# Scores of the 1024 noisy keys in one two-bank PSUM tile: PSUM as two double tiles and four single banks

## The chip, the cores and the metric

The kernel runs on one core of one Trainium2 chip. A time is the device time of one execution in microseconds (us). TensorE (PE) does the matrix products and the transposes, VectorE (DVE), ScalarE (ACT) and GpSimd (POOL) the rest, and SyncE (SP) issues the DMAs. PE writes its results to PSUM, which has eight banks of 512 float32 numbers in each of 128 partitions; DVE and ACT read them from there.

## The reference

A two-layer transformer trunk: 1024 noisy tokens (`x`) and 256 context tokens (`ctx`), width 1024, in float32. Each layer is a mixer with two kinds of attention heads, an output projection, and a SwiGLU of hidden width 2816. The part that matters here:

```
s = einsum('bqhgd,bkhd->bhgqk', q, k) * scale      # keys: 256 context and 1024 noisy ones
p = softmax(s, axis=-1)
o = einsum('bhgqk,bkhd->bqhgd', p, v)
...
s = einsum('bqhid,bkhid->bhiqk', q, k) * d ** -0.5 # differential heads: two streams i
p = softmax(s, axis=-1)
a = p[:, :, 0] - lam * p[:, :, 1]
...
g, u = split(h @ w_in, 2); y = (silu(g) * u) @ w_out
```

Layer 0 has eight windowed heads with sinks (A) and eight latent heads over all 1280 keys (B). Layer 1 has eight grouped heads (C) and four differential heads (D), both over all 1280 keys.

## The kernel before

Activations lie feature by feature, in chunks of tokens: `a` and `b` (512 noisy tokens each) and `c` (256 context tokens, layer 0 only). Every float32 operand is split into a high and a low float32r part, and a product is three matmuls (`mm3`).

**The order.** The program is first recorded by `Recorder` (L51). It then issues the instructions as a list schedule orders them: each engine takes, of the instructions whose operands are there, the first in program order, with estimated times and with the number of buffers of each pool counted (`room`, L196). This fixes each engine's order at build time. The tile framework then sets every wait: a reader waits for the writers of its tile, a later writer for the readers before it, and a new tile for the last readers of the buffer that it gets.

**PSUM.** Before, one pool `pb` (L283) has eight tiles of one bank each; `pr.b()` (L309) takes one. Who takes them:

- `Proj.run` (L783): 24 matmuls into one bank, then an ACT copy.
- Attention, a `Job` (L792) of up to four query tiles of 128. `scores` (L842) makes, per query tile and stream, three pieces (noisy keys 0 to 511, 512 to 1023, context keys), each in its own bank with its own DVE maximum (`piece`, L852); a small DVE maximum joins the three. `ex` (L867) then makes three ACT exponentials with sums. Windowed jobs (`s_local`, L935) use a bank of up to 384 columns and one of 256 per query tile.
- `pv_steps` (L988): for each of ten key tiles four transposes of probabilities into a bank (`tr`), an ACT cast to the high part, a DVE subtraction for the low part (`low`), and two products with the values into the job's output bank, which is held for the whole job.
- `g_ada` (L437): one bank is held over 32 matmuls that are spread beside the attention.
- `gu` (L1631): for hidden tile j and chunk c, 24 matmuls into a bank for g and 24 into another for u. ACT takes Silu of g and DVE multiplies it with u. `down` (L1649): eight banks in turn, three matmuls each, and a DVE addition to the running sum from each.

The full-key jobs are 16 of B, 8 of D (two streams each) and 16 of C: 192 score steps. `gu` runs 22 times for each chunk: 66 times in layer 0 (a, b, c), 44 in layer 1 (a, b).

Of the kernel before, what the change touches and what calls it, by code (L numbers as in the profile page):

```python
# [32 lines left out]
# columns of the packed per-partition parameters  # L33
# [17 lines left out]
class Recorder:  # L51
    """Stands for nc while the program is laid out. The instructions are then issued as a list schedule orders them:
    an engine that is free takes, of the instructions whose operands are there, the first in program order.
    Times are estimates that only decide the order; Tile sets every wait."""
# [27 lines left out]
    def boxes(ap):  # L82
        """Tile name and the boxes (rows, columns) that ap covers."""
# [44 lines left out]
    def record(self, k, f, name, args, kw):  # L128
# [46 lines left out]
        # from the engine of the row to the engine of the column  # L175
# [87 lines left out]
class FM:  # L263
    """Feature-major activations of one token chunk: [128, KT, n] over 4 KB tiles."""
# [11 lines left out]
class Prog:  # L276
    def __init__(self, ctx, nc, tc, d, out):
# [5 lines left out]
        self.pb = ctx.enter_context(tc.tile_pool(name="pb", bufs=8, space=bass.MemoryType.PSUM))  # L283
        self.dp = ctx.enter_context(tc.tile_pool(name="dp", bufs=1, space=bass.MemoryType.DRAM))
        for p, n in (("sp", 24), ("tp", 44), ("up", 13), ("pb", 8)):
            nc.pool(p, n)
# [24 lines left out]

    def dram(self, shape, dt=F32R):
        return self.dp.tile(shape, dt, name=self.nm("scr"))
# [90 lines left out]
    def mm3(self, ps, terms):  # L404
        """sum over terms (whi, wlo, xhi, xlo) of w^T x."""
# [6 lines left out]
    def wsplit(self, raw, w=1024):  # L412
        """The first w columns of a weight tile, split."""
# [23 lines left out]
    def g_ada(self, l, g, ahead=2):  # L437
        """The 2048 modulation columns of group g."""
# [37 lines left out]
    def derive(self, l, g):  # L476
        """Scales and gates with the norms' gains: A1, G1, A2, G2 per feature and stream."""
# [28 lines left out]
        # first guess from the exponent, then three Newton steps  # L506
# [8 lines left out]
    def expand(self, cols):  # L515
        """Columns [128, w], each 64 times in a row."""
# [5 lines left out]
    def bcast(self, cols, g=1):  # L522
        """Token columns [128, nt * g] to rows: [128, n tokens] in PSUM."""
# [8 lines left out]
    def sq_add(self, acc, x, n, k):  # L532
        """x^2, the k-th term, to the sums acc (one on Pool, a second one on DVE)."""
# [17 lines left out]
    def g_modnorm(self, x, n, A, Bv, put, acc=None, w=1):  # L551
        """rms-normalised x times A plus B, split; A(kt), B(kt) are per-partition columns."""
# [1299 lines left out]
```

## Time and profile before

| | |
|---|---|
| median of 3 runs | 3406.78 us (3404.93 to 3407.7) |
| profiled execution, span from first to last instruction | 3405.7 us |
| PE busy | 3302.8 us (97%) |
| DVE busy | 2079.6 us (61%) |
| ACT busy | 1398.0 us (41%) |
| POOL busy | 697.2 us (20%) |

The profiled execution is told by its span; what lies around the span is not shown, and its 3405.7 us lie inside the range of the runs. A busy PE in such a profile is one whose modelled matmul records leave no gap. The stages as read from the trace: start, norms and projections of layer 0 up to about 295 us, windowed attention (A) to 467, latent attention (B) to 746, output projection, norms and SwiGLU of layer 0 to about 1720, projections of layer 1 to 2100, differential attention (D) to 2308, grouped attention (C) to 2554, output projection and SwiGLU of layer 1 to the end.

### The profile page before, as it was taken

What the parts mean: (1) busy time and instruction counts of PE and PEld (TensorE: products, weight loads), DVE (VectorE), ACT (ScalarE), POOL (GpSimd) and SP (SyncE); (2) the same over time, 40 slices, a digit from 0 to 9 for tenths busy, and PEclk for the clock granted to TensorE, in tenths of its full rate; (3) what the DMA queues carried; (4) which work ended last, traced back from release to release, by engine and by line L of the source; (5) the groups of instructions that cost most, each with busy time, mean ns of one, the idle gap of its engine ahead of it and who ended that gap; (6) DMA issues with size and microseconds to landing.
All of it is one profiled execution on the core that took longest, in us unless ns stands there. A gap on an engine that the chain in (4) does not pass through costs nothing.

```text
span 3405.7 us, 45603 instructions
## 1 busy us (share of the span) xinstructions
PE 3302.8 (97%) x16916; PEld 2687.9 (79%) x16916; DVE 2079.6 (61%) x4013; ACT 1398.0 (41%) x3200; POOL 697.2 (20%) x1059
## 2 busy tenths in 40 slices
PE   7989999999999999999998999999999999999997
PEld 5865588887888888888877895678887788888886
DVE  5565588875534444444468745898994545444545
ACT  4365688874411111111134324788994411111111
POOL 2311221125200000000044723682114200000003
PEclk8999999999999999999999999999999999999998
DMA  6266442354201111111123346412145211111111
GB/s 236 81 236 229 167 132 72 98 193 160 80 28 42 44 38 38 38 38 38 38 95 136 105 133 194 130 52 71 60 163 176 68 56 38 56 43 51 56 56 62
DMA packets 134446, 325.56 MB, mean 96 GB/s; under 512 B 12432, under 2 KB 34640, under 8 KB 134224
## 3 DMA queue, kind: packets, MB, share of 16 engines
q1 hardware_dynamic: 134224, 322.65, 28.8%
q8 instruction: 133, 2.18, 0.3%
q14 instruction: 89, 0.73, 0.1%
HBM read 243.63 MB, written 71.63 MB: 93 GB/s over the span
## 4 chain that ended last, share of the span: by engine, by line
PE 82%; DVE 8%; POOL 3%; DMA 3%; ACT 2%; issue 2%; POOLq 0%; SPq 0%; DVEq 0%; ACTq 0%
PE b L260 82%; DVE T L260 3%; DVE U L260 3%; DVE S L260 2%; POOL S L260 2%; POOL U L260 1%; ACT T L260 1%; DMA scr<-T 1%; ACT U L260 1%; DMA T<-in_ada_w_dram 1%; DMA U<-scr 1%; POOL T L260 0%; DMA T<-in_ctxT_dram 0%; POOLq L1847 0%; DMA T<-scr 0%
## 5 line engine op out<-in xcount | busy, mean ns | idle before, releaser
L260 PE MATMUL b<-T,T 128*128 128x512 f32 (+5 forms) x9958 | 2170.5, 367 | 23.1 <-DVE T L260 9.6
L260 PEld LDWEIGHTS b<-T,T 128*128 128x128 f32 (+2 forms) x9958 | 1714.3, 190 | 378.9 <-issue 27.9
L260 PE MATMUL b<-U,T 128*128 128x512 f32 (+2 forms) x3808 | 946.0, 381 | 9.4 <-DVE U L260 4.4
L260 PEld LDWEIGHTS b<-U,T 128*128 128x128 f32 x3808 | 661.6, 190 | 135.6 <-issue 12.8
L260 POOL TENSOR_TENSOR U<-U,U 128x512 f32<-128x512 f32 (+1 forms) x130 | 174.9, 1349 | 1696.5 <-ACT U L260 1692.2
L260 DVE TENSOR_TENSOR T<-T,b 128x512 f32<-128x512 f32 (+1 forms) x872 | 501.6, 631 | 11.4 <-PE b L260 6.5
L260 DVE TENSOR_TENSOR T<-T,T 128x1024 fp32r<-128x1024 f32 (+4 forms) x274 | 316.7, 1170 | 227.3 <-PE b L260 172.9
L260 DVE TENSOR_REDUCE S<-b 128x1 f32<-128x512 f32 (+1 forms) x672 | 377.3, 571 | 116.2 <-PE b L260 111.0
L260 DVE TENSOR_TENSOR U<-U,b 128x512 f32<-128x512 f32 (+1 forms) x118 | 75.2, 637 | 608.4 <-PE b L260 605.5
L260 ACT ACTIVATE T<-b,S 128x512 f32<-128x512 f32 (+1 forms) x640 | 390.6, 616 | 53.5 <-DVE S L260 36.0
L260 ACT CAST T<-T 128x1024 fp32r<-128x1024 f32 (+4 forms) x234 | 225.1, 968 | 360.8 <-PE b L260 296.4
L260 DVE TENSOR_TENSOR U<-b,U 128x512 fp32r<-128x512 f32 (+3 forms) x528 | 335.6, 648 | 21.2 <-ACT U L260 16.8
L260 ACT ACTIVATE U<-b 128x256 f32<-128x256 f32 (+1 forms) x148 | 81.3, 552 | 620.8 <-PE b L260 618.8
L260 ACT CAST U<-b 128x512 fp32r<-128x512 f32 (+3 forms) x528 | 295.7, 572 | 97.4 <-PE b L260 90.4
L260 PE MATMUL b<-ident,T 128*128 128x128 f32 x1968 | 314.3, 276 | 6.3 <-DVE U L260 2.5
L260 PEld LDWEIGHTS b<-ident,T 128*128 128x128 f32 x1968 | 239.7, 141 | 76.0 <-ACT T L260 9.3
L260 ACT CAST U<-U 128x512 fp32r<-128x512 f32 (+1 forms) x110 | 63.6, 578 | 305.1 <-DVE U L260 300.9
L260 POOL TENSOR_TENSOR T<-T,T 128x512 f32<-128x512 f32 (+2 forms) x104 | 132.5, 1282 | 175.6 <-ACT T L260 162.4
L260 PE MATMUL b<-T,silc 128*32 128x512 f32 x384 | 131.8, 626 | 11.0 <-DMA T<-in_ada_w_dram 10.5
L260 DVE TENSOR_TENSOR U<-U,U 128x512 fp32r<-128x512 f32 (+4 forms) x167 | 118.9, 713 | 38.2 <-POOL U L260 27.1
L260 ACT ACTIVATION_READ_ACCUMULATOR T<-b,S 128x1 f32 x640 | 136.6, 213 | 0.0
L260 ACT ACTIVATE U<-T 128x512 f32<-128x512 f32 (+1 forms) x174 | 96.4, 578 | 96.1 <-DVE T L260 90.4
(71 smaller groups left out, 1514.5 us busy)
## 6 DMA issues: line engine op xcount, KB each, us to landing
scr<-T SPq DMA_DIRECT2D x114, 512.0 KB
T<-in_ada_w_dram SPq DMA_DIRECT2D x96, 512.0 KB
T<-in_ffn_in_dram SPq DMA_DIRECT2D x88, 512.0 KB
T<-scr SPq DMA_DIRECT2D x82, 512.0 KB
T<-scr SPq DMA_DIRECT2D x88, 256.0 KB
T<-in_ffn_out_dram SPq DMA_DIRECT2D x44, 512.0 KB
T<-in_w_out_dram SPq DMA_DIRECT2D x32, 512.0 KB
T<-scr SPq DMA_DIRECT2D x72, 128.0 KB
```

What stands on the lines that cost most here:

```text
L260: f(*args, **kw)
```

## The change

The scores with the 1024 noisy keys go to one tile of two banks, with one DVE maximum over 1024 columns and one ACT exponential over 1024 columns; the context scores keep a single bank. To make room, PSUM becomes a pool `pb` of four single banks and a pool `pw` of two double tiles. `Proj.run` now takes a double tile (and uses half of it), and `gu` puts g and u into the two halves of one double tile. All else takes single banks, as before: transposes, output sums, context and windowed scores, `down`, `g_ada`, the norms.

```diff
-        self.pb = ctx.enter_context(tc.tile_pool(name="pb", bufs=8, space=bass.MemoryType.PSUM))
+        self.pb = ctx.enter_context(tc.tile_pool(name="pb", bufs=4, space=bass.MemoryType.PSUM))
+        self.pw = ctx.enter_context(tc.tile_pool(name="pw", bufs=2, space=bass.MemoryType.PSUM))
...
+    def w(self):
+
+        return self.nc.tile("pw", self.pw.tile([P, 1024], F32, tag="w", name=self.nm("w")))
...
-            ps = pr.b()
+            ps = pr.w()
...
-        parts = (("x", 0, 512), ("x", 512, 1024), ("c", 0, 256)) if self.full else (("c", 0, 256),)
...
+        def x(h):
+            if h == 0:
+                own["s"] = pr.w()
+            self.mms(si, qi, "x", h * 512, h * 512 + 512, own["s"][:, h * 512:h * 512 + 512])
+            if h == 0:
+                return None
+            return lambda: nc.vector.tensor_reduce(out=m[:, mo:mo + 1], in_=own["s"], axis=AX.X, op=ALU.max)
+
+        def ctx():
+            s = own["sc"] = self.mms(si, qi, "c", 0, 256)
...
+            last = i == int(full)
+            nc.scalar.activation(own["c"] if last else own["x"], own.pop("sc") if last else own.pop("s"), AF.Exp,
+                                 bias=neg, accum_out=z[:, zo + i:zo + i + 1])
...
+        if full:
+            return [lambda: x(0), lambda: x(1), ctx], [lambda: ex(0), lambda: ex(1)]
...
-        ps = {}
-        for kind in "gu":
+        ps, both = {}, pr.w()
+        for i, kind in enumerate("gu"):
             wh, wl = self.conv[kind, j]
-            ps[kind] = pr.b()[:, :n]
+            ps[kind] = both[:, i * 512:i * 512 + n]
```

The order of the built programs shows what else moves. The first place is PE at the middle of one `gu` of layer 0 with 512 tokens, where the matmuls of g end and those of u begin (`b` and `w` are PSUM tiles, the other names SBUF tiles). Before:

```order
L260 MATMUL b3061_3142<-T2525_2606,T3009_3090 128x512
L260 MATMUL b3061_3142<-T2529_2610,T3009_3090 128x512
L260 MATMUL b3061_3142<-T2525_2606,T3010_3091 128x512
L260 MATMUL b3062_3143<-T2522_2603,T3011_3092 128x512 [waits DVE_49]
L260 MATMUL b3062_3143<-T2526_2607,T3011_3092 128x512
L260 MATMUL b3062_3143<-T2522_2603,T3012_3093 128x512
```

The same place now:

```order
L260 MATMUL w2962_3046<-T2458_2542,T2913_2997 128x512
L260 MATMUL w2962_3046<-T2462_2546,T2913_2997 128x512
L260 MATMUL w2962_3046<-T2458_2542,T2914_2998 128x512
L260 MATMUL w2962_3046<-T2455_2539,T2915_2999 128x512
L260 MATMUL w2962_3046<-T2459_2543,T2915_2999 128x512 [waits Activation_49]
L260 MATMUL w2962_3046<-T2455_2539,T2916_3000 128x512
```

The second matmul of u has got a wait for ACT. Followed through the counts of the semaphores in the built program, the awaited instruction is the Silu that reads the first half of the same tile, and that Silu waits for the first matmul of u, the last PE write to the tile ahead of it in the order. Of the 110 runs of `gu`, 109 have such a wait inside their 48 matmuls: 87 with 512 tokens, 22 with 256 (there mostly at the third matmul of u). Before, none has.

The second place is PE in the windowed attention, around the job whose output bank is `b983` (`ident` marks transposes; `b894` is the bank of `g_ada`; 128x384 and 128x256 from two `T` tiles are windowed and context scores). Before:

```order
L260 MATMUL b984_1065<-T794_875,T797_878 128x384 [waits PE_49]
L260 MATMUL b984_1065<-T795_876,T797_878 128x384
L260 MATMUL b986_1067<-ident_75,T938_1019 128x128 [waits DVE_49]
L260 MATMUL b986_1067<-ident_75,T949_1030 128x128
L260 MATMUL b894_975<-T946_1027,silc_81 32x512 [waits DMAHW7_49]
L260 MATMUL b894_975<-T946_1027,silc_81 32x512
L260 MATMUL b983_1064<-U977_1058,T34_115 128x384 [waits Activation_49]
L260 MATMUL b894_975<-T947_1028,silc_81 32x512 [waits DMAHW0_49]
L260 MATMUL b989_1070<-T796_877,T797_878 128x256 [waits DVE_49]
```

Now:

```order
L260 MATMUL b983_1067<-U981_1065,T35_119 128x384 [waits Activation_49]
L260 MATMUL b984_1068<-T794_878,T797_881 128x384 [waits DVE_49]
L260 MATMUL b984_1068<-T795_879,T797_881 128x384
L260 MATMUL b983_1067<-U982_1066,T35_119 128x384
L260 MATMUL b986_1070<-ident_78,T938_1022 128x128 [waits Activation_49]
L260 MATMUL b986_1070<-ident_78,T949_1033 128x128
L260 MATMUL b989_1073<-T796_880,T797_881 128x256 [waits DVE_49]
L260 MATMUL b989_1073<-T796_880,T797_881 128x256
L260 MATMUL b983_1067<-U987_1071,T35_119 128x256 [waits Activation_49]
L260 MATMUL b990_1074<-ident_78,T949_1033 128x128 [waits DVE_49]
```

The matmuls of `g_ada` are gone from here (they stand earlier, closer together), and each new tile (`b984`, `b986`, `b989`, `b990`) waits for a reader of a tile that was written just ahead of it.

The third place is DVE in the grouped attention. Before, a score step has three wide maxima and a small one:

```order
L260 TENSOR_REDUCE S5537_5620<-b5545_5628 128x1 [waits PE_49]
L260 TENSOR_REDUCE S5481_5564<-S5480_5563 128x4 [waits Activation_49]
L260 TENSOR_TENSOR T5431_5514<-T5431_5514,b5548_5631 128x512 [waits PE_49]
L260 TENSOR_REDUCE S5537_5620<-b5549_5632 128x1 [waits PE_49]
L260 RECIPROCAL S4005_4088<-S5481_5564 128x4 [waits DVE_49]
L260 TENSOR_REDUCE S5537_5620<-b5554_5637 128x1 [waits PE_49]
L260 TENSOR_REDUCE S5536_5619<-S5537_5620 128x1 [waits DVE_49]
```

Now it has two and a small one:

```order
L260 TENSOR_REDUCE S5287_5373<-w5302_5388 128x1 [waits PE_49]
L260 TENSOR_TENSOR U5305_5391<-b5303_5389,U5304_5390 128x512 [waits Activation_49]
L260 TENSOR_REDUCE S5287_5373<-b5311_5397 128x1 [waits PE_49]
L260 TENSOR_TENSOR U5310_5396<-b5308_5394,U5309_5395 128x512 [waits Activation_49]
L260 TENSOR_REDUCE S5286_5372<-S5287_5373 128x1 [waits DVE_49]
```

One wide maximum per step is gone from DVE; the one that stays reads both banks (`w5302`).

## Rows read from the trace of the kernel before

**Rows 1.** The page: span, busy time by engine, then the chain that ended last.
```profile
span 3405.7 us, 45603 instructions
PE 3302.8 (97%) x16916; PEld 2687.9 (79%) x16916; DVE 2079.6 (61%) x4013; ACT 1398.0 (41%) x3200; POOL 697.2 (20%) x1059
...
PE 82%; DVE 8%; POOL 3%; DMA 3%; ACT 2%; issue 2%; POOLq 0%; SPq 0%; DVEq 0%; ACTq 0%
```

**Rows 2.** Busy time by stretch: A, B, most of D, C, both SwiGLU stages.
```profile
core 0: us, PE busy (x) PEld busy (x) DVE busy (x) ACT busy (x) POOL busy (x), PEclk, DMA share, GB/s
295.00:467.00 172.00, 167.04 (x873) 105.76 (x874) 107.03 (x367) 114.62 (x368) 44.24 (x73) 0.97 0.58 185
467.00:746.00 279.00, 276.34 (x1681) 236.17 (x1680) 233.75 (x486) 231.01 (x612) 46.29 (x51) 1.00 0.41 118
2145.00:2308.00 163.00, 159.76 (x842) 119.09 (x840) 153.68 (x383) 129.53 (x364) 134.07 (x196) 0.98 0.23 69
2308.00:2554.00 246.00, 242.40 (x1465) 202.65 (x1464) 227.32 (x470) 224.85 (x580) 41.64 (x58) 1.00 0.31 101
900.00:1720.00 820.00, 820.00 (x4306) 709.05 (x4306) 379.54 (x652) 142.65 (x215) 9.53 (x30) 1.00 0.12 40
2690.00:3355.00 665.00, 665.00 (x2946) 551.04 (x2945) 321.91 (x468) 120.07 (x159) 6.92 (x16) 1.00 0.16 50
```

**Rows 3.** Timeline, one gu and the start of its down, 512 tokens, layer 0.
```profile
start us, us, engine line op out<-in xcount [idle before <-releaser]
1202.61 11.07 PE L260 MATMUL b<-T,T 128*128 128x512 f32 x48
...
1208.28 0.60 ACT L260 ACTIVATE U<-b 128x512 f32<-128x512 f32 x1 [7.06 <-PE b L260]
...
1213.79 0.69 DVE L260 TENSOR_TENSOR U<-U,b 128x512 f32<-128x512 f32 x1 [10.03 <-PE b L260]
```

**Rows 4.** Timeline near 231 us: PE waits for an ACT read of PSUM.
```profile
231.34 0.58 ACT L260 COPY U<-b 128x512 f32<-128x512 f32 x1
...
231.97 0.96 PE L260 MATMUL b<-T,T 128*128 128x512 f32 x3 [1.43 <-ACT U L260]
```

**Rows 5.** Timeline of layer 1's SwiGLU: three running matmuls; casts around a Silu.
```profile
2903.82 0.84 PE L260 MATMUL b<-T,T 128*128 128x512 f32 x3
...
2913.43 1.05 ACT L260 CAST T<-T 128x1024 fp32r<-128x1024 f32 x1 [2.46 <-DVE T L260]
2915.58 0.60 ACT L260 ACTIVATE U<-b 128x512 f32<-128x512 f32 x1 [1.10 <-PE b L260]
```

**Rows 6.** Timeline of one down with 256 tokens, layer 0.
```profile
1199.73 3.04 PE L260 MATMUL b<-U,T 128*128 128x256 f32 x24
1200.35 0.42 DVE L260 TENSOR_TENSOR U<-U,b 128x256 f32<-128x256 f32 x1 [2.92 <-PE b L260]
1200.69 0.75 DVE L260 TENSOR_TENSOR T<-T,b 128x256 f32<-128x256 f32 x2
...
1201.35 0.42 DVE L260 TENSOR_TENSOR U<-U,U 128x256 fp32r<-128x256 f32 x1
1201.69 2.07 DVE L260 TENSOR_TENSOR T<-T,b 128x256 f32<-128x256 f32 x6
```

**Rows 7.** Groups by form, whole span: count, busy us, mean ns, idle before.
```profile
L260 ACT ACTIVATE T<-b,S 128x512 f32<-128x512 f32 x384 | 265.6, 697 | 47.9 <-DVE S L260 30.5 <-PE b L260 14.6 <-POOL T L260 0.9
L260 DVE TENSOR_REDUCE S<-b 128x1 f32<-128x512 f32 x384 | 261.4, 685 | 58.3 <-PE b L260 55.2
L260 ACT ACTIVATION_READ_ACCUMULATOR T<-b,S 128x1 f32 x640 | 136.6, 213 | 0.0
L260 ACT ACTIVATE T<-b,S 128x256 f32<-128x256 f32 x256 | 126.8, 495 | 5.6 <-DVE S L260 5.5
L260 DVE TENSOR_REDUCE S<-b 128x1 f32<-128x256 f32 x288 | 120.6, 419 | 57.8 <-PE b L260 55.8
L260 ACT ACTIVATE U<-b 128x256 f32<-128x256 f32 x32 | 12.3, 384 | 49.4 <-PE b L260 49.2
```

**Rows 8.** Groups by form, 2411 to 2553 us: output copies, one for each C job.
```profile
L260 ACT COPY U<-b 128x512 f32<-128x512 f32 x10 | 5.9, 591 | 1.9 <-PE b L260 1.9
```

**Rows 9.** Timeline in C: a bank of transposes, its cast, its subtraction.
```profile
2401.85 0.60 PE L260 MATMUL b<-ident,T 128*128 128x128 f32 x4
...
2402.53 0.63 ACT L260 CAST U<-b 128x512 fp32r<-128x512 f32 x1
...
2403.55 0.68 DVE L260 TENSOR_TENSOR U<-b,U 128x512 fp32r<-128x512 f32 x1
```

**Rows 10.** Groups by form, 444.3 to 467.4 us: output copies, one for each A job.
```profile
L260 ACT COPY U<-b 128x512 f32<-128x512 f32 x3 | 1.8, 587 | 1.4 <-PE b L260 0.8 <-issue 0.6
```

**Rows 11.** Timeline in A: transposes, context scores, and readers of PSUM tiles.
```profile
445.18 0.38 PE L260 MATMUL b<-ident,T 128*128 128x128 f32 x2
...
445.31 0.48 PE L260 MATMUL b<-T,T 128*128 128x256 f32 x2
...
445.40 0.55 DVE L260 CUSTOM_DVE_ANT_0 T<-b,U 128x384 f32<-128x384 f32 x1
445.42 0.47 ACT L260 CAST U<-b 128x384 fp32r<-128x384 f32 x1
...
445.94 0.55 DVE L260 TENSOR_TENSOR U<-b,U 128x384 fp32r<-128x384 f32 x1
445.98 0.47 ACT L260 ACTIVATE T<-b,S 128x256 f32<-128x256 f32 x1
```

More of the change, by code (lines that the diff above doesn't have):

```diff
@@ L847, in scores @@
         neg = self.neg[:, 8 * si + qi:8 * si + qi + 1]
-        parts = (("x", 0, 512), ("x", 512, 1024), ("c", 0, 256)) if self.full else (("c", 0, 256),)
-        np_ = len(parts)
+        full = self.full
         own = {}
-        def piece(i):
-            s = self.mms(si, qi, *parts[i])
-            st.append(s)
+        def x(h):
[5 more added lines that the diff above has]
+            return lambda: nc.vector.tensor_reduce(out=m[:, mo:mo + 1], in_=own["s"], axis=AX.X, op=ALU.max)
@@ L856, in mx @@
+        def ctx():
+            s = own["sc"] = self.mms(si, qi, "c", 0, 256)
             def mx():
-                if np_ == 1 and not self.sinks:
+                if not full and not self.sinks:
                     nc.vector.tensor_reduce(out=neg, in_=s, axis=AX.X, op=ALU.max, negate=True)
                     return
-                o = mo + i if np_ > 1 else mo + 1
-                nc.vector.tensor_reduce(out=m[:, o:o + 1], in_=s, axis=AX.X, op=ALU.max)
-                if i == np_ - 1:
-                    nc.vector.tensor_reduce(out=neg, in_=m[:, mo + (np_ == 1):mo + 3], axis=AX.X, op=ALU.max,
-                                            negate=True)
@@ L865, in piece, with place @@
-            return mx
+                nc.vector.tensor_reduce(out=m[:, mo + 1:mo + 2], in_=s, axis=AX.X, op=ALU.max)
+                o = mo if full else mo + 1
+                nc.vector.tensor_reduce(out=neg, in_=m[:, o:o + 2], axis=AX.X, op=ALU.max, negate=True)
+            return mx
+        def place():
+            if self.neglam is not None:
+                if si == 0:
+                    self.zd = pr.S()
+                own["z"], own["o"] = self.zd, 4 * si
+            else:
+                own["z"], own["o"] = self.z, 4 * qi
+            if si == 0:
+                own["x"] = pr.T() if full else None
+                self.pb.append(own["x"])
+                own["c"] = self.pc[:, qi * 256:(qi + 1) * 256]
+            else:
+                own["x"], own["c"] = pr.T(), pr.U()[:, :256]
@@ L867, in ex @@
         def ex(i):
-            kind, a, b = parts[i]
             if i == 0:
-                if self.neglam is not None:
-                    if si == 0:
-                        self.zd = pr.S()
-                    own["z"], own["o"] = self.zd, 4 * si
-                else:
-                    own["z"], own["o"] = self.z, 4 * qi
-                if si == 0:
-                    own["x"] = pr.T() if self.full else None
-                    self.pb.append(own["x"])
-                    own["c"] = self.pc[:, qi * 256:(qi + 1) * 256]
-                else:
-                    own["x"], own["c"] = pr.T(), pr.U()[:, :256]
@@ L882, in ex @@
-            z, zo = own["z"], own["o"]
-            nc.scalar.activation(own["x"][:, a:b] if kind == "x" else own["c"], st[i], AF.Exp, bias=neg,
-                                 accum_out=z[:, zo + i:zo + i + 1])
-            if i == np_ - 1:
-                st.clear()
-                if si == 1:
-                    self.combine(qi, own["x"], own["c"], z)
-        return [lambda i=i: piece(i) for i in range(np_)], [lambda i=i: ex(i) for i in range(np_)]
+                place()
+            z, zo = own["z"], own["o"]
@@ L892, in combine @@
+            last = i == int(full)
+            nc.scalar.activation(own["c"] if last else own["x"], own.pop("sc") if last else own.pop("s"), AF.Exp,
+                                 bias=neg, accum_out=z[:, zo + i:zo + i + 1])
+            if last and si == 1:
+                self.combine(qi, own["x"], own["c"], z)
+        if full:
+            return [lambda: x(0), lambda: x(1), ctx], [lambda: ex(0), lambda: ex(1)]
+        return [ctx], [lambda: ex(0)]
     def combine(self, qi, pb1, pc1, s):
@@ L895, in combine @@
         z = s[:, 8:10]
-        nc.vector.tensor_reduce(out=z, in_=s[:, 0:8].rearrange("p (s t) -> p s t", s=2)[:, :, 0:3], axis=AX.X,
+        nc.vector.tensor_reduce(out=z, in_=s[:, 0:8].rearrange("p (s t) -> p s t", s=2)[:, :, 0:2], axis=AX.X,
                                 op=ALU.add)
@@ L913, in sums @@
         if self.neglam is None:
-            w = 3 if self.full else 1 if self.local is None else 2
+            w = 1 if not self.full and self.local is None else 2
             if w == 1:
```

7 lines of the change are left out of this document (3 added, 4 removed).

## The prediction

> **What bounds the kernel now.** I read the page first: PE is busy for 3302.8 of 3405.7 us, and 82% of the chain that ended last is PE [rows 1]. Then the stretches, since the change touches stages with different limits [rows 2]. In the two SwiGLU stretches PE has no gap at all (820.00 of 820 and 665.00 of 665 us), while DVE is busy 46 to 48% and ACT 17 to 18% of them: there the time is PE's, DVE or ACT time that is saved gives nothing, and each wait put in front of a matmul costs its full length. In C all three engines are nearly full (PE 242.40, DVE 227.32, ACT 224.85 of 246 us). In D DVE leads (153.68 of 163 us in the part shown, much of the rest idle at its start). In A and B PE leads again, with DVE and ACT at 62 to 84%.
>
> **What is removed.** Each of the 192 full score steps loses one wide DVE maximum and one ACT exponential with its read of the sum. A maximum takes 0.685 us on 512 columns and 0.419 on 256 [rows 7], so a column costs about 1.04 ns and the start 0.15 us: one over 1024 columns is about 1.22 us, against 2 x 0.685. Saved: 0.15 us, 29 us in all. An exponential takes 0.697 and 0.495 us, and the read of its sum 0.213 [rows 7]: one over 1024 columns is about 1.10 + 0.21, against 2 x 0.91, so 0.51 us less, 98 us in all (less in place, since the read overlaps). That is the whole gift, and nearly all of it lies beside PE work. Only in D, where DVE sets the pace, can it come out directly: 64 steps x 0.15 = 10 us at most.
>
> **What is added in gu.** This is the largest term, and it stands in the order: PE may not issue the second matmul of u (the third with 256 tokens) before Silu has read g, and Silu itself waits for the first matmul of u. The stall is one round trip PE, ACT, PE. In the trace the 48 matmuls of a gu run in 11.07 us [rows 3]; with 0.39 us for one (three in a row take 0.84 [rows 5]) they start every 0.227 us. The 24th then ends at about 1208.23, and Silu starts at 1208.28: 0.05 us after it. Silu takes 0.60 us [rows 3]. Where PE waits for an ACT read of PSUM, it starts 0.05 us after that read ends (231.34 + 0.58 to 231.97), and its next three matmuls take 0.96 us where running ones take 0.84 [rows 4, 5]: 0.12 us for starting again. So the second matmul of u starts 0.39 + 0.05 + 0.60 + 0.05 = 1.09 us after the first instead of 0.227, and with the restart a gu of 512 tokens loses 0.98 us. With 256 tokens matmuls start every 0.12 us and last 0.28 (3.04 us for 24 [rows 6]), and an ACT read of 256 columns takes 0.384 [rows 7]: 0.28 + 0.05 + 0.38 + 0.05 - 0.12 + 0.12 = 0.76 us. The order has 87 and 22 of them: 85 + 17 = **+102 us**. Nothing lies beside it: the other accumulations of these stages come later in PE's order, and PE issues in order. Queued behind the waiting matmul are the rest of u and the down products; DVE's multiplication waits for these and is late by as much. Bounds: without the restart, and with handovers of 0.04, 0.83 x 87 + 0.62 x 22 = 86; if the weight casts of 1.05 us, which today end about a microsecond ahead of Silu [rows 5], hold it up once in ten times, 112.
>
> The Trainium skill, PSUM — Partial Sum Buffer (PSUM bank collisions raise a hardware error), says that two engines may use PSUM at the same time as long as they are in different banks, and g and u are in different banks of the double tile. By that rule alone this term is zero and the sum below ends near 3439. The rows of before agree with it, since there PE goes on with u while Silu reads g [rows 3]; but the order now has the wait, so I count by the order.
>
> **Down with four banks.** With 256 tokens a bank is filled every 0.36 us, and DVE frees one every 0.33 (six in 2.07 us, the last lasting 0.42), after a multiplication and with a subtraction between [rows 6]. With four banks the fifth fill (1.44 us after the start, at 1201.17) finds the first addition done (about 1201.1), the sixth (1201.53) the second, but the seventh (at 1201.89) needs the third addition, which starts at 1201.69 and takes 0.42: some 0.3 us of waiting, 22 times, **+6 us** (0 to 15). With 512 tokens a bank is filled every 0.69 us and an addition is as long, with half a microsecond to spare: nothing.
>
> **Attention with four single banks.** The output bank is held throughout, so three are left for scores and transposes (two while a group of g_ada runs).
>
> A: per job (three in 23.1 us, 7.7 us each [rows 10]) seven transposed tiles, four context and four windowed scores pass through them. A transposed tile is held for its transposes, cast and subtraction, 0.38 + 0.47 + 0.55 and three handovers, 1.55 us; context scores for matmuls, maximum, small maximum and exponential, about 0.48 + 0.42 + 0.15 + 0.47 + 0.2 = 1.7; windowed scores 1.1 [rows 7, 11]. Together 22.5 us of bank time, 7.5 us over three banks, if no reader is ever late. ACT and DVE are busy for most of the job, so some lateness is certain; a quarter more makes 9.4 us, 1.7 x 16 jobs = 27. PE's matmuls for g_ada fill part. I take **+18** (0 to 38).
>
> C: a job takes 14.2 us (ten in 142 [rows 8]). A transposed tile is held from 2401.85 to 2404.23, 2.4 us [rows 9]; context scores, for which the exponential of the 1024 comes first, about 3.8 us by the durations above. 14.2 for the output, 4 x 3.8 and 10 x 2.4 make 53 of the 57 us of bank time that four banks have in a job: 94% full, and the readers' longest pieces have grown to 1.2 and 1.3 us. Against it stand 2 us of ACT and 0.6 us of DVE less per job, of some 13 of each (227 and 225 of 246 us [rows 2]). I take 0.5 us more per job, **+8** (-10 to +20).
>
> B: the same bank time in jobs of about 16 us, 86% full: **+2** (-8 to +12). D: jobs of 26 us leave room, except while g_ada holds a bank; DVE's saving against that: **-4** (-10 to +10).
>
> **The rest.** Proj.run takes two double tiles where eight were free; a tile takes 5 us to fill and its ACT copy 0.6, so two are enough, except where norms still deliver. The norms hold a single bank for their broadcast while down runs on the others. **+4** (0 to 12).
>
> Sum: 102 + 6 + 18 + 8 + 2 - 4 + 4 = 136; 3405.7 + 136 = 3541.7, and as the median of the runs is 1.1 us above the profiled span, 3542.
>
> **The rivals.**
> 1. *The wait in gu costs nothing and the saving counts: faster.* Its place is the second matmul of u, its price zero if Silu's end never comes after that matmul's turn. For it: the saving in D and C is real, 10 + 10 us, and if bank waits stay at their low bounds (0 in A, -8 in B) the time is 3407 - 28 = 3379. Against it: Silu alone takes 2.6 matmul intervals [rows 3] and starts after a matmul that PE has just issued. It decides only if the round trip of 1.09 us were under 0.3. 2%.
> 2. *The change does not do this:* the stall is hidden because PE finds other work in its order, and bank shortage and saving cancel: within a few us of 3407. The order shows nothing between the two matmuls. 2%.
> 3. *Banks starve the attention:* A, B and C each lose 15 to 20% more than I take, (172 + 279 + 246) x 0.17 = 118 more less what I have counted, about 90 us more: 3632. For it: all first writes in A wait for a reader in the order shown, and ACT and DVE are 90% full in C. Against it: g_ada and the scores in double tiles give PE other work. 10%.
> 4. *The clock falls.* The stretches with the largest PE gaps show a granted clock under 1 (A 0.97, D 0.98), C with 3.6 us of gaps in 246 shows 1.00 [rows 2]. If the 109 stalls pulled PE down to 1.2 GHz for a tenth of the 1485 us of SwiGLU, that is 75 us more: 3617. The Trainium skill, TensorE: Matmul & The Clock Gate (A second HAM failure mode: psum-queue depth-cycling), tells of a kernel whose short pauses between groups of matmuls made the clock go back and forth. In C there are such pauses and no fall, so the trace speaks against it here. 4%.
> 5. *The round trip stands, attention gains:* with A, B, C and D at their low bounds the sum is 102 + 6 - 28 + 4 = 84: 3491. 12%.
>
> **How the numbers follow.** My case, round trip and mild bank shortage, has 70%, and its own time is 3542. Its bounds (86 to 112 for gu, 0 to 15 for down, the attention terms not all at one end) give 3500 to 3590. The range of 8 in 10 reaches a little towards cases 5 and 3: 3490 to 3595. A measurement can tell a change from none at about 0.2%, 7 us. Faster than that comes only from rival 1 (2%), the same from 2 (2%), and slower is the rest, 96%.
>
> **What will show it.** In the SwiGLU stretches PE has gaps for the first time, some 109 of about 0.7 us before a matmul of w, ended by ACT, and each hidden tile of layer 1 (two chunks) takes about 2 us longer; layer 0's SwiGLU grows by about 67 us, layer 1's by 43. Silu starts one matmul later in its gu. The maxima and exponentials of 1024 columns take about 1.2 and 1.1 us. In A, PE gaps ended by DVE and ACT grow and the windowed stage takes some 190 us; C takes some 254, D some 4 us less. The prediction is wrong if the SwiGLU stretches have no gaps, if the stall is twice the round trip (a second wait in gu), or if the attention stages move by over 30 us together in either direction from what I take.

## The result and the profile after

The changed kernel takes 3599.56 us (median of 4 runs, 3594.81 to 3602.75), the kernel before 3405.99 us on the same chip: a ratio of 1.057, 95% interval 1.0557 to 1.0583. The time lies 4.6 us above the predicted range (3490 to 3595); the change costs 193.6 us where 136 were forecast. One of the four runs of experiment 5 below, 3804 us at a lower granted clock, is left out of its interval.

The page of the changed kernel, its lines as in [rows 1]:

```profile
span 3595.7 us, 45029 instructions
PE 3343.3 (93%) x16916; PEld 2683.2 (75%) x16916; DVE 2083.2 (58%) x3821; ACT 1363.9 (38%) x2818; POOL 699.9 (19%) x1059
...
PE 63%; DVE 6%; ACT 4%; POOL 3%; issue 2%; DMA 1%; POOLq 0%; SPq 0%; ACTq 0%; DVEq 0%
```

PE's idle time in the profiled execution went from 102.9 to 252.4 us, and PE's share of the chain from 82 to 63%. To see where, I cut both traces at the same events: the ACT copies that end attention jobs, the first and last cast of an activation in each SwiGLU, and the last value product.

| stretch | before, us | after, us | change | forecast |
|---|---|---|---|---|
| start to A | 238.9 | 238.1 | -0.8 | |
| A | 228.7 | 283.0 | +54.3 | +18 |
| B | 278.2 | 285.8 | +7.6 | +2 |
| output projection, norms, layer 0 | 132.7 | 131.9 | -0.8 | rest: +4 in all |
| SwiGLU, layer 0 | 912.0 | 961.5 | +49.5 | +67 |
| projections and values, layer 1 | 270.2 | 288.4 | +18.2 | rest |
| D | 264.9 | 270.1 | +5.2 | -4 |
| C | 227.8 | 243.3 | +15.5 | +8 |
| output projection, norms, layer 1 | 121.2 | 122.6 | +1.4 | rest |
| SwiGLU, layer 1 | 696.7 | 736.6 | +39.9 | +43 |
| end | 34.5 | 34.5 | 0 | |

The changes sum to 190.0 us, the difference of the two spans. These are the stretches A, B, SwiGLU, projections, D, C and SwiGLU of the changed kernel (columns as in [rows 2]):

```profile
238.10:521.10 283.00, 236.59 (x1181) 144.31 (x1179) 157.27 (x504) 162.38 (x499) 49.33 (x87) 0.95 0.51 166
521.10:806.90 285.80, 280.68 (x1683) 234.54 (x1682) 228.49 (x419) 218.84 (x484) 47.73 (x51) 1.00 0.39 113
938.80:1900.30 961.50, 918.90 (x4709) 773.56 (x4707) 451.09 (x773) 175.45 (x276) 48.48 (x83) 1.00 0.13 43
1900.30:2188.70 288.40, 264.52 (x1419) 231.94 (x1420) 181.49 (x305) 86.76 (x180) 124.78 (x221) 0.95 0.35 114
2188.70:2458.80 270.10, 238.89 (x1235) 164.85 (x1234) 214.96 (x469) 171.20 (x387) 179.25 (x251) 0.96 0.39 121
2458.80:2702.10 243.30, 234.96 (x1372) 188.47 (x1370) 210.61 (x382) 197.76 (x427) 37.42 (x43) 1.00 0.29 94
2824.70:3561.30 736.60, 705.45 (x3069) 570.14 (x3070) 346.27 (x502) 129.05 (x177) 18.39 (x33) 1.00 0.15 50
```

PE, which had no gap inside the SwiGLU of [rows 2], is idle there for 42.6 and 31.2 us; in A for 46.4. DVE and ACT are not the bound in A (157 and 162 of 283 us): PE waits for readers of PSUM, on engines that are idle much of the time.

PE's waits in the changed kernel, first in the two SwiGLU stretches, then in A (engine, tile, whom it waited for: us in all, times, longest):

```profile
PE w L260 <- ACT U L260: 39.8, 64, 0.7
...
PE w L260 <- ACT U L260: 30.9, 42, 2.6
...
PE b L260 <- ACT U L260: 18.5, 31, 6.8
PE b L260 <- DVE S L260: 11.9, 27, 0.9
```

And one `gu` of the changed kernel in the timeline, which answers to [rows 3]:

```profile
1326.10 5.66 PE L260 MATMUL w<-T,T 128*128 128x512 f32 x24
...
1331.80 0.60 ACT L260 ACTIVATE U<-w 128x512 f32<-128x512 f32 x1 [7.68 <-PE w L260]
...
1332.45 5.51 PE L260 MATMUL w<-T,T 128*128 128x512 f32 x23 [0.69 <-ACT U L260]
```

(The trace lacks one of the 48 matmuls.) PE has issued u's first matmul, the last of the first row, and stops. Silu starts 0.04 us after that matmul's end, takes 0.60, and PE goes on 0.05 us after Silu with the other 23 of u. Over the whole trace there are 87 such stops with 512 columns (median 0.69, mean 0.73 us) and 22 with 256 (median 0.47, mean 0.54): the 109 of the order, 75.0 us.

The wide readers, by form:

```profile
L260 DVE TENSOR_REDUCE S<-w 128x1 f32<-128x1024 f32 x192 | 233.9, 1218 | 37.1 <-PE w L260 36.7
...
L260 ACT ACTIVATE T<-w,S 128x1024 f32<-128x1024 f32 x192 | 214.9, 1119 | 56.9 <-DVE S L260 46.5
```

They last 1218 and 1119 ns, as worked out from [rows 7].

### The profile page after: what moved, and what is told of

It is laid out like the page before. It is cut to its first block, busy times and chain, and to the rows that moved or that the text cites. A ratio compares the mean times of both kernels' runs of the same rounds, so it can differ in the third digit from the quotient of the medians.

```text
span 3595.7 us, 45029 instructions
## 1 busy us (share of the span) xinstructions
PE 3343.3 (93%) x16916; PEld 2683.2 (75%) x16916; DVE 2083.2 (58%) x3821; ACT 1363.9 (38%) x2818; POOL 699.9 (19%) x1059
## 4 chain that ended last, share of the span: by engine, by line
PE 63%; DVE 6%; ACT 4%; POOL 3%; issue 2%; DMA 1%; POOLq 0%; SPq 0%; ACTq 0%; DVEq 0%
PE w L260 39%; PE b L260 24%; ACT U L260 3%; DVE T L260 3%; DVE U L260 2%; POOL S L260 1%; POOL U L260 1%; ACT T L260 1%; DVE S L260 1%; DMA T<-scr 1%; DMA T<-in_ada_w_dram 0%; POOL T L260 0%; DMA T<-U 0%; ACT L260 0%; POOLq L1858 0%
## 5 line engine op out<-in xcount | busy, mean ns | idle before, releaser
L260 PE MATMUL w<-T,T 128*128 128x512 f32 (+2 forms) x8600 | 1958.0, 377 | 100.2 <-ACT U L260 75.0
L260 PEld LDWEIGHTS w<-T,T 128*128 128x128 f32 (+1 forms) x8600 | 1494.5, 190 | 427.9 <-ACT U L260 120.1
L260 DVE TENSOR_TENSOR U<-U,w 128x512 f32<-128x512 f32 (+1 forms) x110 | 69.7, 634 | 691.5 <-PE w L260 691.5
L260 PE MATMUL b<-ident,T 128*128 128x128 f32 x1968 | 315.0, 279 | 22.5 <-DVE S L260 7.8
L260 ACT ACTIVATE U<-w 128x256 f32<-128x256 f32 (+1 forms) x130 | 72.0, 554 | 642.0 <-PE w L260 640.2
L260 PE MATMUL b<-T,T 128*128 128x320 f32 (+4 forms) x1358 | 268.7, 323 | 19.3 <-ACT U L260 7.4
L260 PEld LDWEIGHTS b<-T,T 128*128 128x128 f32 (+1 forms) x1358 | 215.8, 192 | 77.8 <-ACT U L260 16.0
L260 DVE TENSOR_REDUCE S<-w 128x1 f32<-128x1024 f32 x192 | 233.9, 1218 | 37.1 <-PE w L260 36.7
L260 ACT ACTIVATE T<-w,S 128x1024 f32<-128x1024 f32 x192 | 214.9, 1119 | 56.9 <-DVE S L260 46.5
L260 POOL TENSOR_TENSOR T<-T,T 128x512 f32<-128x512 f32 (+2 forms) x104 | 131.9, 1278 | 246.1 <-ACT T L260 231.0
L260 DVE TENSOR_REDUCE S<-b 128x1 f32<-128x256 f32 x288 | 119.8, 418 | 71.3 <-PE b L260 70.5
```

The costliest lines, as they stand in the source:

```text
L260: f(*args, **kw)
```

## The experiments

Medians and ratios are against the kernel before, which ran beside each group of kernels (3403.2 to 3403.8 us). The table gives the stretches that the texts speak of; "proj." is layer 1's projections and values. Some expectations count by earlier cuts: A from 295 us (172 us before, 226 changed), D from its first copy (225 and 241), layer 1's projections up to that copy (318 changed).

| kernel | median, us | ratio, 95% interval | A | B | SwiGLU 0 | proj. | D | C | SwiGLU 1 |
|---|---|---|---|---|---|---|---|---|---|
| before, 8 single banks | 3406 | 1 | 228.7 | 278.2 | 912.0 | 270.2 | 264.9 | 227.8 | 696.7 |
| changed, 4 single, 2 double | 3600 | 1.057 | 283.0 | 285.8 | 961.5 | 288.4 | 270.1 | 243.3 | 736.6 |
| 1 Silu behind u | 3508 | 1.0289-1.0320 | 283.8 | 286.6 | 902.3 | 295.0 | 272.1 | 243.3 | 699.7 |
| 2 g and u apart | 3498 | 1.0259-1.0293 | 282.9 | 286.3 | 907.6 | 288.3 | 269.1 | 243.7 | 698.0 |
| 3 halved readers | 3674 | 1.0778-1.0810 | 286.0 | 312.2 | 960.9 | 287.4 | 293.7 | 262.6 | 736.6 |
| 4 windowed scores in doubles | 3594 | 1.0543-1.0574 | 278.3 | 286.0 | 961.0 | 287.4 | 272.0 | 243.1 | 736.6 |
| 5 and A's context scores | 3570 | 1.0466-1.0501 | 251.7 | 287.0 | 961.7 | 288.4 | 272.4 | 243.3 | 736.6 |
| 6 before with 5 single | 3691 | 1.0826-1.0858 | 249.3 | 342.4 | 914.6 | 281.4 | 349.5 | 317.1 | 703.8 |
| 7 changed with 3 single | 3912 | 1.1479-1.1515 | 415.9 | 347.5 | 963.9 | 289.5 | 317.4 | 322.6 | 738.8 |
| 8 as 2, projections in singles | 3505 | 1.0277-1.0311 | 283.5 | 284.7 | 905.7 | 285.2 | 272.0 | 243.7 | 698.2 |
| 9 modulation in D later | 3602 | 1.0567-1.0599 | 283.5 | 288.9 | 961.4 | 288.5 | 270.3 | 243.2 | 736.6 |
| 10 = 2, 5 and 9 together | 3470 | 1.0171-1.0205 | 250.3 | 287.2 | 909.0 | 287.2 | 270.5 | 243.4 | 698.0 |
| 11 6 single, 1 double | 3454 | 1.0129-1.0159 | 237.3 | 279.2 | 912.4 | 276.0 | 276.1 | 238.4 | 702.7 |
| 12 = 11, some of A in the double | 3452 | 1.0132-1.0162 | 238.4 | 279.9 | 912.1 | 276.3 | 276.9 | 238.4 | 701.9 |

**1. Silu behind u.** In `Recorder.record`, a read of a double tile counts as a read of all of it, so that Silu is ordered behind u:

```diff
+            whole = [(0, P, 0, 1024)] if not w and self.pool_of.get(t) == "pw" else None
-            for b in self.boxes(a):
+            for b in whole or self.boxes(a):
```

> The changed kernel, but Silu is issued only behind u's last matmul, so g and u still share one double tile and no matmul of u has a reader of g ahead of it. Theory (the wait for a reader of the same tile is the price of gu): the two SwiGLU stretches give back their 90 us, layer 0's from 961 to about 912 us between its first and last cast, layer 1's from 737 to about 697, the other stages stay, and the whole comes to about 3510 us (3500 to 3520). Rival (the price is that only two double tiles exist, and PE waits until the multiplication gives one back): Silu and the multiplication now come later by up to 5 us, a tile is held longer, and the SwiGLU stretches stay or grow: 3600 us or more.

**2. g and u apart**, each in half of a double tile of its own:

```diff
-            ps[kind] = both[:, i * 512:i * 512 + n]
+            ps[kind] = pr.w()[:, :n]
```

> The changed kernel, but g and u take a double tile each (half of each unused). Theory (a reader in the same tile): the stall is gone, with a few us left where gu follows gu without down products between them, as both double tiles are then still held: 3512 us (3502 to 3530). Rival (too few double tiles): each gu now needs both, so PE waits for the multiplication before every gu: 3600 to 3800 us.

Both did what the theory said. The two SwiGLU stretches, first with Silu behind u:

```profile
942.60:1844.80 902.20, 900.44 (x4702) 775.94 (x4700) 445.13 (x773) 177.47 (x276) 46.41 (x79) 1.00 0.14 44
2773.20:3472.80 699.60, 695.41 (x3066) 574.78 (x3065) 344.24 (x502) 130.23 (x176) 20.09 (x34) 1.00 0.17 53
```

then with g and u apart:

```profile
939.70:1847.30 907.60, 902.60 (x4709) 777.26 (x4707) 450.87 (x773) 176.56 (x277) 48.67 (x83) 1.00 0.14 46
2766.80:3464.80 698.00, 697.40 (x3085) 576.94 (x3085) 346.28 (x502) 129.13 (x176) 18.05 (x33) 1.00 0.17 53
```

PE's gaps are gone in both (0.6 to 5.0 us left where 42.6 and 31.2 were), and with them 92.5 us (apart: 53.9 and 38.6). With Silu behind u the stretches give back 59.2 and 36.9 us. The first keeps the shared tile and mends only the order; the second keeps the order of readers and takes another tile, of which there are no more than before. So the price was the reader of g ahead of u's second matmul, and two double tiles are enough for `gu`: the rival falls.

**3. Halved readers.** Two maxima and two exponentials of 512 columns read the double tile (the maximum of the context scores and the sums take one more column):

```diff
-            return lambda: nc.vector.tensor_reduce(out=m[:, mo:mo + 1], in_=own["s"], axis=AX.X, op=ALU.max)
+                for k in range(2):
+                    nc.vector.tensor_reduce(out=m[:, mo + k:mo + k + 1], in_=own["s"][:, k * 512:k * 512 + 512],
+                                            axis=AX.X, op=ALU.max)
...
+                    nc.scalar.activation(own["x"][:, h], s[:, h], AF.Exp, bias=neg,
+                                         accum_out=z[:, zo + k:zo + k + 1])
```

> The changed kernel, but the full scores in their double tile are read by two maxima and two exponentials of 512 columns, as before the change, so that only the use of PSUM is left of the change there. Theory (attention loses by four single banks, and the wide pieces save what their start costs): B, C and D each get longer by 3 to 8 us, A stays, 3610 us (3600 to 3625). Rival (attention loses because the pieces of 1.2 and 1.3 us hold up the other readers of PSUM on DVE and ACT): B and C go back to about 279 and 248 us, 3575 us (3565 to 3590).

It took 3674 us, 74.5 more than the changed kernel: both expectations missed. I had 3 to 8 us for each of B, C and D. B, D and C with halved readers:

```profile
527.40:839.60 312.20, 288.04 (x1678) 232.00 (x1677) 238.01 (x481) 233.79 (x612) 46.05 (x51) 1.00 0.36 104
2219.80:2513.50 293.70, 246.19 (x1236) 166.82 (x1235) 225.71 (x540) 188.42 (x525) 179.72 (x251) 0.96 0.37 111
2513.50:2776.10 262.60, 243.31 (x1372) 187.03 (x1370) 214.85 (x439) 213.32 (x543) 36.41 (x43) 1.00 0.27 85
```

No engine is fuller than in the changed kernel (in C ACT 81%, DVE 82%), so engine time is not the reason. A step could hold its double tile longer, by 2 x 0.685 - 1.218 = 0.15 us of maxima and 2 x (0.697 + 0.213) - (1.119 + 0.213) = 0.49 us of exponentials [rows 7]: 64 steps x 0.64 over two tiles would be 20 us for each of B, D and C, and measured are 26, 24 and 19. The sizes fit, but the trace shows something else. These are PE's waits for a DVE maximum before a matmul of the double tile, in B, D and C, of which the changed kernel has none:

```profile
PE w L260 <- DVE S L260: 18.0, 30, 0.8
PE w L260 <- DVE S L260: 16.7, 22, 1.1
PE w L260 <- DVE S L260: 9.0, 27, 0.3
```

And one of them in C:

```profile
2604.63 0.40 PE L260 MATMUL w<-T,T 128*128 128x512 f32 x1
...
2605.07 0.69 DVE L260 TENSOR_REDUCE S<-w 128x1 f32<-128x512 f32 x1 [0.28 <-PE w L260]
...
2605.81 0.50 PE L260 MATMUL w<-T,T 128*128 128x512 f32 x1 [0.32 <-DVE S L260]
```

In 131 of the 192 steps of this program the maximum of the first half stands ahead of the last matmul of the second half, in the changed kernel in none: the edit sets up the wait of `gu` a second time, with DVE for ACT. These 43.7 us are nearly all of the 46 us by which PE's idle time grew in the three stages; the other 23 of their 69 us are PE busy time. So this run does not price the wide readers. Whether a longer hold costs anything, and whether the long pieces hold others up, stays open.

**4 and 5. A's scores in the double tiles**, which stand idle in A; 4 moves the windowed scores, 5 the context scores as well:

```diff
-            s = self.mms(0, qi, "x", lo * P, lo * P + w)
+            s = self.mms(0, qi, "x", lo * P, lo * P + w, pr.w()[:, :w])
...
-            s = st["c"] = self.mms(0, qi, "c", 0, 256)
+            s = st["c"] = self.mms(0, qi, "c", 0, 256, pr.w()[:, :256])
```

> The changed kernel, but the windowed scores of A go to the double tiles, which stand idle in A. Theory (A lost 54 us because its transposed tiles, context scores and windowed scores share three single banks): a third of the demand on them goes away, the waits of PE in A fall from 39 us to about 10 and its clock comes back, so A takes about 185 us for 226: 3560 us (3550 to 3575). Rival (A lost by its lower clock or by the order of its readers, not by banks): A stays within 10 us of 226: 3590 to 3605 us.

> The changed kernel with the windowed and the context scores of A in the double tiles, so that only transposed tiles, the output and the modulation groups use the four single banks there. Theory (A lost 54 us by bank time: with the windowed scores alone moved, two banks were still left for 17.6 us of holding per job beside the output and a modulation group): transposed tiles need 10.9 us of two banks in a job of 7.7, so PE's waits in A go from 35 us to about 15 and A takes about 245 us (235 to 255) for 278 to 283: 3560 us. Rival (A is held by something that the banks do not touch): A stays above 270: 3590 us.

The first gave back 4.7 us of A where I expected 40: A stayed within the 10 us of its rival. With the second it was 31.3 us, as expected. A with both moved:

```profile
239.20:490.90 251.70, 230.28 (x1175) 143.35 (x1173) 150.54 (x503) 157.65 (x498) 49.67 (x87) 0.95 0.57 185
```

PE's gaps fell from 46.4 to 21.4 us. So it is banks after all, but not by thirds, as I had counted: taken in this order, the windowed scores bring 5 us and the context scores 27.

**6. Before with five single banks**, and nothing else changed:

```diff
-        self.pb = ctx.enter_context(tc.tile_pool(name="pb", bufs=8, space=bass.MemoryType.PSUM))
+        self.pb = ctx.enter_context(tc.tile_pool(name="pb", bufs=5, space=bass.MemoryType.PSUM))
```

> The kernel before, with five single banks instead of eight and nothing else changed (three banks idle). Theory (bank time in A): A, whose instructions are those of the changed kernel too, takes between 229 and 283 us, about 255; B, C and D, which hold three banks for the scores of a step, get much longer, together by over 100 us; the SwiGLU stretches stay within 10 us of 912 and 697, since nothing waits inside g and u: 3550 to 3650 us. Rival (A's 54 us come from elsewhere): A within 5 us of 229.

**7. The changed kernel with three single banks:**

```diff
-        self.pb = ctx.enter_context(tc.tile_pool(name="pb", bufs=4, space=bass.MemoryType.PSUM))
+        self.pb = ctx.enter_context(tc.tile_pool(name="pb", bufs=3, space=bass.MemoryType.PSUM))
```

> The changed kernel with three single banks instead of four (one bank idle), two double tiles as they are. Theory (single banks limit C and B too, 94 and 86% full by the prediction's count): A above 350 us for 283, C above 275 for 243, B above 305 for 286, the whole over 3720 us. Rival (in C and B the two double tiles limit, since a step holds one from its first matmul to the end of its exponential, as the run with halved readers suggests, where these stages lost 19 and 26 us): C and B stay within 8 us, A and the modulation groups of D alone grow.

A with five single banks, in the kernel before:

```profile
239.00:488.30 249.30, 220.39 (x1165) 143.75 (x1165) 152.84 (x504) 159.31 (x499) 49.06 (x87) 0.94 0.57 188
```

A and C with three, in the changed one:

```profile
241.10:657.00 415.90, 307.43 (x1178) 188.31 (x1178) 163.86 (x504) 165.23 (x498) 49.57 (x87) 0.70 0.35 113
2702.50:3025.10 322.60, 257.06 (x1367) 189.09 (x1368) 220.21 (x383) 202.35 (x431) 37.42 (x43) 0.98 0.22 73
```

With run 11 this makes a scale for A: 228.7 us on eight single banks, 237.3 on six, 249.3 on five, 283.0 on four, 415.9 on three. Run 6 shares only fewer banks with the change, and A gets longer there as the theory had it, so the rival falls; B, C and D lose more than I expected (238 us together), and the whole, 3691 us, lies above the 3550 to 3650. In run 7 C grows by 79 and B by 62 us (the theory's bounds were 32 and 19): the fourth single bank is worth that much to these stages too. What more than four would give them, with two double tiles, no run shows.

**8. Projections back in single banks**, with g and u apart:

```diff
-            ps = pr.w()
+            ps = pr.b()
```

> The changed kernel with g and u in a double tile each, and the projections' products back in single banks. Theory (with two double tiles the projections wait for the copy of the tile before last only where the norms still deliver, and the 17 us that layer 1's projections lost are a chain of norms on GpSimd that started late): within 6 us of the run with g and u apart, 3498 us. Rival (two double tiles hold the projections up): layer 1's stretch from the last cast of layer 0 to the first job falls from 318 back to 310 us or less, 3485 us.

3505 us, 6.6 more than run 2, just outside the 6 that I expected; layer 1's projections take 285.2 for 288.3 us. The two double tiles are not what holds them up. But the chain of norms is not by itself the cause either: the stretch goes with the number of single banks, 270.2 us on eight, 276.0 on six, 281.4 on five, 285.2 to 288.5 on four (295.0 in run 1), and 289.5 on three, without the steep end that A has.

**9. The modulation groups of D two jobs later.** In the changed trace PE stands still early in D for 12.86 us, the longest wait of the stage (columns: start, duration; in brackets the wait before):

```profile
2226.75 1.19 PE L260 MATMUL b<-U,T 128*128 128x512 f32 x4 [1.11 <-DVE U L260]
2240.80 1.92 PE L260 MATMUL b<-T,silc 128*32 128x512 f32 x4 [12.86 <-DMA T<-in_ada_w_dram]
...
2196.65 17.29 SPq L260 DMA_DIRECT2D T<-scr  x14
2223.33 19.75 SPq L260 DMA_DIRECT2D T<-in_ada_w_dram  x5
```

Its weights were issued at 2223.33, behind 14 key loads.

```diff
-            elif hd == 0:
+            elif hd == 1:
                 loadf = lambda: pr.slow.extend(pr.g_ada(1, g) for g in (1, 2))
```

> The changed kernel with the modulation groups of D begun two jobs later, nothing else. Theory (D's loss is one wait of 12.9 us for modulation weights whose load stands in SyncE's queue behind the key loads, not banks): the stretch from the first copy of D to its last output falls from 241 us to about 228, 3587 us in all. Rival (D loses by single banks, as A does): the stretch stays within 4 us or the wait comes back at the later place: 3595 to 3602 us.

The wait is gone, and the first modulation matmul follows its neighbours without a gap:

```profile
2242.73 0.38 PE L260 MATMUL b<-ident,T 128*128 128x128 f32 x2
2243.04 1.04 PE L260 MATMUL b<-T,silc 128*32 128x512 f32 x2
```

D is as long as before the edit (270.3 for 270.1 us), the total 3602. Removing the largest single wait of the stage gave nothing: PE's waits for a double tile grew from 8.0 to 15.9 us in its place, and PE's idle time fell only from 31.2 to 27.2 us. The total is what the rival expected; that single banks are D's cause is not shown. The cut that I used in this expectation, at the first copy, is a modulation copy, so the table cuts at the last value product.

**10. Runs 2, 5 and 9 together** (the edits are theirs).

> The changed kernel with the found costs mended together: g and u in a double tile each, the windowed and context scores of A in the double tiles, and the modulation groups of D begun two jobs later. Theory (the costs are separate and add up): SwiGLU as with g and u apart (908 and 698 us), A about 252, D shorter by the 12.9 us for which PE waited for a load of modulation weights; 3498 - 31 - 10 = about 3457 us (3450 to 3470). Rival (the shortage only moves on, for instance into B, whose jobs follow A's): above 3480 us. Still slower than before: what is left is A's 23, B's 8 and C's 15 us on four single banks.

3470 us; without the 10 us that run 9 did not bring, the sum was 3498 - 31 = 3467. The two costs are separate and add up.

**11 and 12. Six single banks and one double tile**, the double used by every second step only; in 12 also by every second windowed score:

```diff
-        self.pb = ctx.enter_context(tc.tile_pool(name="pb", bufs=4, space=bass.MemoryType.PSUM))
-        self.pw = ctx.enter_context(tc.tile_pool(name="pw", bufs=2, space=bass.MemoryType.PSUM))
+        self.pb = ctx.enter_context(tc.tile_pool(name="pb", bufs=6, space=bass.MemoryType.PSUM))
+        self.pw = ctx.enter_context(tc.tile_pool(name="pw", bufs=1, space=bass.MemoryType.PSUM))
...
+        wide = (si if self.neglam is not None else qi) % 2 == 0
```

> Another split of PSUM: six single banks and one double tile. g, u and the projections use singles as before the change; every second full step (in D every first stream) takes the double tile with one wide maximum and exponential, the others three singles with narrow ones. Theory (the loss of the change is the number of single banks and the wait in gu, and wide readers by themselves save time): A about 238 us on six banks (by 229, 249 and 283 on eight, five and four), B and C within 8 us of 278 and 228, D 2 to 8 us less than 225, SwiGLU 912 and 697: 3405 to 3425 us. Rival (one double tile is held too long and stops PE's order): B and C as in the changed kernel or worse, 3440 us or more.

> The same split, and in A every second windowed score in the double tile, which stands idle there. Theory: A comes back to about 231 us, 3400 to 3418 us in all, the nearest to the kernel before. Rival: A as on six banks, no difference to the run without it.

3454 and 3452 us: the best of the family, 1.4% slower than before. Both totals lie above what I expected, run 11's where its rival had it, and in run 12 A did not come back (238.4 us), as its rival said. A and C of run 11:

```profile
237.70:474.90 237.20, 215.57 (x1168) 138.15 (x1169) 149.54 (x505) 157.72 (x500) 50.00 (x97) 0.98 0.59 197
2349.20:2587.50 238.30, 230.30 (x1357) 185.15 (x1356) 209.22 (x411) 203.10 (x484) 37.79 (x63) 1.00 0.29 93
```

A and B came out as expected (237.3 and 279.2), C and D 10.6 and 11.2 us above the kernel before where I expected nothing and a gain; B speaks against run 11's rival, and C lies between the two. Layer 1's projections and SwiGLU kept 6 us each. No run with wide readers has B, C or D shorter than on eight single banks. With PE at 225 of 228 us in C there was little to win.

## Why the prediction was wrong

**The direction, the wait in gu and its place were right.** The step "0.39 + 0.05 + 0.60 + 0.05 = 1.09 us after the first instead of 0.227" is met: from u's first matmul to its second the median is 1.075 us. The allowance of 0.12 us for starting again was too large: layer 1's SwiGLU gives 39.9 / 44 = 0.91 us for a `gu` of 512 tokens against 0.98. Without the 0.12 us for all 109 stops the sum is 102 - 13 = 89. The whole term measured 89 us against the kernel before (92.5 by run 2), for 102, inside its bounds of 86 to 112. Rivals 1 and 2, and the rule of the Trainium skill's page PSUM — Partial Sum Buffer (PSUM bank collisions raise a hardware error) taken as the price, are refuted by the 109 stops. The rule itself stands: in run 2 PE writes u's bank while ACT reads g's, without a stop (the Silu at 1311.67 us lies inside a row of its matmuls without a gap). What stopped PE was a wait that the program holds per tile, where the rule speaks of banks.

**Down with four banks:** +6 taken, nothing measured: in the changed layer-0 SwiGLU PE waits for DVE's additions for 0.9 us in all, and run 2's stretch is 4.4 us shorter than before the change.

**A: the step that failed.** The prediction put "7.5 us over three banks, if no reader is ever late ... a quarter more makes 9.4 us, 1.7 x 16 jobs = 27" and took +18 with 38 as the upper bound. It measured +54.3, 3.4 us for each job. The mechanism was right, as runs 5 to 7 show; the term was mis-sized, in the holding times first. (The recorded terms also add up to 22.1 us, 7 x 1.55 + 4 x 1.7 + 4 x 1.1, and not to 22.5.) They were least times, from one passage without queues [rows 11]. Following each tile of the changed A from its first matmul to the end of its last reader, I find on average 1.94 us for a transposed tile (121 tiles) where 1.55 was taken, 2.95 for context scores (80 tiles) where 1.7 was taken, and 1.21 for windowed scores (64 tiles) where 1.1 was taken. In the A before, where banks were plenty, they are 3.12, 4.36 and 1.43. With the measured times a job needs 7 x 1.94 + 4 x 2.95 + 4 x 1.21 = 30.2 us of bank time, 10.1 us over three banks where the prediction had 9.4 with its allowance. Against the 7.7 us of a job that is 2.4 x 16 = 38 us, an estimate, where it took 18. Context scores have the largest error (5.0 us a job), and run 5, which moves them out of the single banks, gives back 27 us.

The second error is the modulation groups. The prediction said that two banks are left while a group runs, and then divided by three throughout. A group's bank is held until ACT has copied it. In the kernel before that copy starts within 1.1 us of the last matmul; in the changed A these are the copies,

```profile
305.58 0.59 ACT L260 COPY U<-b 128x512 f32<-128x512 f32 x1
385.99 0.58 ACT L260 COPY U<-b 128x512 f32<-128x512 f32 x1
459.12 0.60 ACT L260 COPY U<-b 128x512 f32<-128x512 f32 x1
```

and the last matmuls end at 290.80, 350.36 and 420.00. So a bank is held from 249 to 306, from 327 to 387 and from 400 to 460 us, 176 of 283 us, and for 90 of these it only waits for the copy. What that costs no run shows, and it is not the whole: from the DVE reading of the 52nd of the 64 windowed scores to its end, where no group holds a bank, A takes 47.7 us (473.4 to 521.1) for 33.9 before (433.6 to 467.5), 4.6 more for each of the three jobs whose scores are left, where 1.7 was counted.

Part of the 54 us is not waiting: PE is "busy" for 236.6 us with the same work as in 216.9 before, at a granted clock of 0.95 after 0.98. By these clocks at most (1 - 0.95) x 283.0 - (1 - 0.98) x 228.7 = 10 us of the 19.7 would be the clock's, an estimate; in run 6, at 0.94, PE is busy for 220.4 us. The rest of that busy time stays open.

**The rest, +4 (0 to 12):** layer 1's projections alone took +18.2. The prediction looked at the two double tiles, which run 8 clears. The stretch follows the number of single banks from eight to four; which of their users it is (broadcasts, sums of squares, norms of queries and keys) stays open.

**B, C and D** had +6 together and measured +28 (7.6, 15.5, 5.2). C's bank count of 94% named the danger; half a microsecond a job should have been one (15.5 / 16). What the 15.5 us are is open: with six single banks and one double tile (run 11) C still keeps 10.6. D's saving of DVE time did not come out. What D's 5 us are was not settled: taking away the wait for the modulation load (run 9) did not bring them back.

Against the sum of 136 the errors are A +36, the rest +14, C, D and B +22, gu -12 and down -6: 54, as 190 against 136. The 18 us of `gu` and `down` hide a part of the miss. By the prediction's own words, attention stages over 30 us from what it takes make it wrong, and they are 59 us off. Rival 3, banks starving the attention, had the right mechanism and 10%; its 118 us over A, B and C became 77, most of it in A.

Rival 4, a falling clock in SwiGLU, did not happen: 109 pauses, and a granted clock of 1.00 in both SwiGLU stretches. The page TensorE: Matmul & The Clock Gate (A second HAM failure mode: psum-queue depth-cycling) of the Trainium skill tells of such a fall in another kernel; this trace does not show it for its pauses, of 0.47 and 0.69 us in the median.

## What to carry to other kernels

When two results are put in one tile to save an instruction, every reader of one becomes a wait for the other's writer: look for what stands between them in the writer's order, or let the reader wait for both (run 1 gave back 92 us with no other change; run 3 walked into the same wait on DVE). When a pool shrinks, size it by holding times that include the wait for readers, subtract each long-lived holder until its last reader is done, and try one tile fewer and one more: the scale is flat first and steep then (A: 237, 249, 283, 416 us on six, five, four, three). And a long wait in a trace has no price until its removal has been timed: taking away 12.86 us in D gave nothing.

## What the runs showed of the hardware that was not expected

- PE's granted clock in A was lower in most runs with more idle time there, but not in step with it: 0.98 before, where PE is busy 95% of the stretch; 0.98 in run 11 and 0.95 in run 5, both at 91%; 0.94 in run 6 at 88%; 0.95 in the changed kernel at 84%; 0.70 in run 7 at 74% (with the two levels of 1.2 and 2.4 GHz, some 60% of that stretch at the lower). In layer 0's SwiGLU 42.6 us of idle time, 39.8 of them in 64 pauses of at most 0.7 us, left it at 1.00.
- Reading 1024 columns of PSUM over two banks in one instruction took 1218 ns for a maximum against 685 for 512 columns, and 1119 for an exponential against 697: within 2% of what a column and the start cost by [rows 7], so nothing is added for the second bank. The saving on the engine was as forecast; what it is worth in time no run here shows by itself.
